# The spread of the output norm's roots as two full-width products, with its steps moved later in the dense work

## The chip, the cores and the metric

The kernel runs on one core of a Trainium2 chip. The metric is the device time of one execution in microseconds (us), as a median of several executions. All arithmetic is in 32-bit floats; a matmul that must be nearly exact in fp32 is written as three products of "high" and "low" parts in the faster type fp32r.

## The reference

One layer of a hybrid encoder is applied to a prompt of 2048 tokens and to a sample of 512 tokens, each with 16 meta tokens ahead of it:

```
u = RMSNorm(h);  proj = u @ w_in          # q, k, v, z of two branches, two merge gates
o_a = neighbourhood attention (8 rows x 16 columns of a 64-wide grid, 2-D bias)
o_b = window attention (+-128 tokens, grouped queries, T5 bias, a sink per head)
y_a = (o_a * silu(z_a)) @ w_proj_a;  y_b = (o_b * silu(z_b)) @ w_proj_b
h   = h + (sigmoid(g_a) * y_a + sigmoid(g_b) * y_b) @ w_out
out = RMSNorm(h)[without the meta tokens]  # x * rsqrt(mean(x*x) + 1e-6) * final_g
```

The change concerns the last line: the sums of squares of h for each token, the root of each, and the multiplication of h by it. The width of h is 1024.

## The kernel before, in words

The 2560 tokens are cut into five windows of 512 (window 0 is the sample). The first part of the kernel, up to about 1190 us, makes all projections, with most of their products in a scheme of seven instead of eight block products, and stores q, k, v, z and the gates in DRAM. The second part, which the change touches, runs over `units` of attention: for each window 32 units of branch a and then 16 of branch b. A unit has stages, and each pass of the main loop takes one unit's loads, another's scores (`s`, lines 1117 and 1118 for branch a, 1223 and 1224 for b), the normalisation of a third (`pr` and `prs`, lines 1058 to 1065), the transposes of a fourth (`tp`, lines 1141, 1243 and 1246, whose results are split into `ph` on ScalarE and `pl` on VectorE, lines 1144/1145 and 1250/1251) and the products with v of a fifth (`oa` and `ob`).

Between these stages TensorE does the dense work, in small steps: a generator yields after each six matmuls of 512 columns (lines 146 to 148). `fill(share)` takes as many steps as are due: one before and one after a unit's transposes in branch b, one per pass in branch a. Steps that a phase has left over are carried into the next (`chain`). The phases are, for each window w:

- beside branch a of window w: `dense_pb(w-1)` (16 steps, tile `psb`, with the loaded gates `sgb`), then `dense_out(w-1)` for the first four of eight output tiles (16 steps, `pso`);
- beside branch b of window w: `dense_out(w-1)` for the last four (16 steps), then `dense_pa(w)` (16 steps, `psa`, gates `sga`), and woven into these by `with_fill` the generator `dense_fin(w-1)`.

`dense_out` leaves for each output tile f the sum h times final_g in `hT`, and adds the square of h into `ssq` on GpSimd (line 1359). `dense_fin(w)`, which runs four times, then makes the norm: `sums` multiplies four 128-token pieces of `ssq` with a column of ones (TensorE, line 170, into the PSUM tile `fin_v`), `rsqrt` finds the roots for 128 x 4 tokens in some 13 small VectorE instructions (lines 153 to 163), `diagonal` puts them on four 128 x 128 diagonals (VectorE, line 177), `spread` multiplies ones with these so that every partition holds all 512 roots (TensorE, line 185, into the PSUM tile `rs_rb`), ScalarE copies them to `rbs` (line 1369), and GpSimd multiplies the eight `hT` by `rbs` (line 1373), each followed by a store to the output through SP's DMA queue.

TensorE's order is the order in which the program issues its instructions (a manual schedule). The other engines and SP's queue are ordered by a planner that simulates the kernel while it builds it. PSUM tiles of one tag share slots: the tag `tp` has three, and serves the transposes (two tiles for a unit of b with three key blocks, one for a unit of a), the scores of every third unit of a, `fin_v` and `rs_rb`. A new tile of a tag waits until all readers of the slot's old tile are done. The gate, residual and output-gate tiles (`sg`) have three slots in SBUF.

After the last unit `finish_end` does the last window's `psb` and its output product `pse`, token-major, with `w_out` halves (`woh`, `wol`) that it loads at that point through SP's queue.

Of the kernel before, what the change touches and what calls it, by code (L numbers as in the profile page):

```python
# [9 lines left out]
F32 = mybir.dt.float32  # L10
F32R = mybir.dt.float32r
# [6 lines left out]
P = 128  # L18
# [7 lines left out]
WTOK = 512  # L26
# [69 lines left out]
def encoder_block(ctx: ExitStack, tc: tile.TileContext, xT, x_end, w_in, w_pa, w_pb, w_o, norm_g, final_g,  # L96
                  final_row, bias_a0, bias_a1, bias_a2, bias_a3, bias_b, bias_b0, outT_p, outT_s, out_e):
    nc = tc.nc
# [23 lines left out]
    def f32(ap):  # L122
        return ap.bitcast(F32)
# [17 lines left out]
    def move(out, in_):  # L141
        last_move[0] = nc.sync.dma_start(*(f32(a) if a.dtype == F32R else a for a in (out, in_)))
        return last_move[0]
# [6 lines left out]
    def rsqrt(small, sq, m, nc_):  # L150

        ve, hv, r, t = (small.tile([P, 8], F32, tag=f"rs{i}", name=f"rs{i}")[:m, :nc_] for i in range(4))
        nc.vector.tensor_scalar(ve, sq, 1.0 / D_MODEL, EPS, ALU.mult, ALU.add)
        nc.vector.tensor_scalar(r.bitcast(I32), ve.bitcast(I32), 1, None, ALU.arith_shift_right)
        nc.vector.tensor_scalar(r.bitcast(I32), r.bitcast(I32), -1.0, float(0x5F3759DF), ALU.mult, ALU.add)
        nc.vector.tensor_scalar(hv, ve, -0.5, None, ALU.mult)
        for _ in range(3):
            if nc_ == 1:
                nc.vector.scalar_tensor_tensor(t, r, hv, r, ALU.mult, ALU.mult)
            else:  # L160
                nc.vector.tensor_mul(t, r, hv)
                nc.vector.tensor_mul(t, t, r)
            nc.vector.scalar_tensor_tensor(r, t, 1.5, r, ALU.add, ALU.mult)
        return r

    def sums(ssq, c0, m, nc_, psum, tag):

        v = psum.tile([P, WTOK], F32, tag=tag, name="fin_v")
        for c in range(nc_):
            nc.tensor.matmul(v[:m, c : c + 1], ssq[:, c0 + c * m : c0 + (c + 1) * m], ones[:, 0:1],  # L170
                             start=True, stop=True)
        return v[:m, :nc_]

    def diagonal(dg, r, m, eng=nc.vector):

        nc_ = r.shape[1]
        eng.tensor_mul(dg[:m, : nc_ * m].rearrange("p (c n) -> p c n", n=m),
                             ident[:m, None, :m].broadcast_to([m, nc_, m]),
                             r[:m, :, None].broadcast_to([m, nc_, m]))

    def spread(psum, tag, dg, m, nc_):

        rb = psum.tile([P, WTOK], F32, tag=tag, name="rs_rb")
        for c in range(nc_):
            nc.tensor.matmul(rb[:, c * P : c * P + m], ones[:m, :], dg[:m, c * m : c * m + m], start=True, stop=True)
        return rb

    def by_ones(psum, tag, h, l, name):

        v = psum.tile([P, WTOK], F32, tag=tag, name=name)  # L190
        nc.tensor.matmul(v, ones_r, h, start=True, stop=False)
        nc.tensor.matmul(v, ones_r, l, start=False, stop=True)
        return v
# [1090 lines left out]
    pools = {}  # L1284
# [7 lines left out]
    def open_dense():  # L1292
        last.close()
        for i, name, bufs in ("d", "dn", 2), ("m", "mp", 1):
            pools[i] = ctx.enter_context(tc.tile_pool(name=name, bufs=bufs, side="right", reuse_waits="tile"))
# [8 lines left out]
    def dense_pa(w):  # L1304
        yh, yl = ys["a", w]
        for f in range(KT):
            if f % 2 == 0:
                wt = weights.next()
            sg = gated("sga", g_d["a", w, f])
            ps = ps_d.tile([P, WTOK], F32, tag="d", name="psa")  # L1310
            for k in range(4):
                s = slice((4 * (f % 2) + k) * P, (4 * (f % 2) + k + 1) * P)
                mm3(ps, wt[:, 0, s], wt[:, 1, s], yh[:, k, :], yl[:, k, :], k == 0, k == 3)
                if k % 2:
                    yield
            ta = acc["t", w, f] = pools["m"].tile([P, WTOK], F32, tag=f"mh{f}", name="ta")
            nc.vector.tensor_mul(ta, ps, sg)

    def dense_pb(w):
        yh, yl = ys["b", w]  # L1320
        acc["m", w] = []
        for f in range(KT):
            if f % 2 == 0:
                wt = weights.next()
            sg = gated("sgb", g_d["b", w, f])
            ps = ps_d.tile([P, WTOK], F32, tag="d", name="psb")
            for k in range(4):
                s = slice((4 * (f % 2) + k) * P, (4 * (f % 2) + k + 1) * P)
                mm3(ps, wt[:, 0, s], wt[:, 1, s], yh[:, k, :], yl[:, k, :], k == 0, k == 3)
                if k % 2:  # L1330
                    yield
            nc.vector.tensor_mul(sg, ps, sg)
            nc.gpsimd.tensor_add(sg, sg, acc["t", w, f])
            mh, ml = (pools["m"].tile([P, WTOK], F32R, tag=f"m{i}{f}", name=f"m{i}") for i in "hl")
            acc["m", w].append((mh, ml))
            nc.scalar.copy(mh, sg)
            nc.gpsimd.tensor_sub(ml, sg, f32(mh))

    def dense_out(w, fs):
        if fs[0] == 0:  # L1340
            acc["s", w] = pools["d"].tile([P, WTOK], F32, tag="ssq", name="ssq", bufs=1)
        ssq = acc["s", w]
        for f in fs:
            wt = weights.next()
            x = gated("xres", xT[f * P : (f + 1) * P, w * WTOK : (w + 1) * WTOK])
            ps = ps_d.tile([P, WTOK], F32, tag="d", name="pso")
            for k in range(KT):
                s = slice(k * P, (k + 1) * P)
                mm3(ps, wt[:, 0, s], wt[:, 1, s], *acc["m", w][k], k == 0, k == KT - 1)
                if k % 2:  # L1350
                    yield
            hT = acc["h", w, f] = pools["m"].tile([P, WTOK], F32, tag="hT", name="hT", bufs=8)
            nc.vector.tensor_add(hT, ps, x)
            nc.scalar.activation(x, hT, AF.Square)
            nc.scalar.mul(hT, hT, fg[:, f : f + 1])
            if f == 0:
                nc.gpsimd.tensor_copy(ssq, x)
            else:
                nc.gpsimd.tensor_add(ssq, ssq, x)

    def dense_fin(w):
        r = rsqrt(pools["d"], sums(acc["s", w], 0, P, 4, ps_p, "tp"), P, 4)
        dg = pools["d"].tile([P, WTOK], F32, tag="rbs", name="rs_dg", bufs=1)
        diagonal(dg, r, P)
        for _ in range(5):
            yield
        rb = spread(ps_p, "tp", dg, P, 4)
        rbs = pools["d"].tile([P, WTOK], F32, tag="rbs", name="rbs", bufs=1)
        nc.scalar.copy(rbs, rb)
        for f in range(KT):  # L1370
            hT = acc["h", w, f]
            with tc.issue_after(low[0]):
                nc.gpsimd.tensor_mul(hT, hT, rbs)
            dst = outT_s if w == 0 else outT_p
            c0 = 0 if w == 0 else (w - 1) * WTOK
            move(dst[f * P : (f + 1) * P, c0 : c0 + WTOK], hT)
            yield
# [98 lines left out]
    def with_fill(main, fill):  # L1476

        for _ in main:
            yield
            next(fill, None)  # L1480
        for _ in fill:
            yield

    def phases(w, br):

        if br == "a":
            if w == 0:
                yield from islice(gates, GATES_A)
            else:
                yield from dense_pb(w - 1)  # L1490
                yield from dense_out(w - 1, range(0, 4))
        elif w == 0:
            yield from gates
            open_dense()
            yield from dense_pa(0)
        else:
            yield from dense_out(w - 1, range(4, 8))
            pa = dense_pa(w)
            yield from islice(pa, 1)
            yield from with_fill(pa, dense_fin(w - 1))  # L1500


# [27 lines left out]
    ps_p = ctx.enter_context(tc.tile_pool(name="ps_p", bufs=3, space=PSUM))  # L1530
# [9 lines left out]
    with tc.manual_schedule(engines={E.PE}):  # L1540
# [22 lines left out]
        for i in range(N):  # L1563
            br, w, _, weight = units[i]
# [128 lines left out]
```

## Time and profile before

| what | value |
|---|---|
| median of 3 runs | 1886.56 us (1884.48 to 1887.48) |
| the profiled execution's own time | 1884.6 us |
| its span in the profile | 1882.6 us |
| TensorE busy | 1857.5 us (99%) |
| VectorE busy | 1326.1 us (70%) |
| ScalarE busy | 1144.5 us (61%) |
| GpSimd busy | 729.2 us (39%) |
| mean granted TensorE clock | 0.998 |
| DMA | 414.35 MB, mean 220 GB/s |

In the profile PE is TensorE's matmuls and PEld its weight loads, DVE is VectorE, ACT ScalarE, POOL GpSimd, and SP issues the DMAs. A row of a timeline has the start in us from the span's start, the duration, the engine, the line of the kernel, the operation, the tiles out<-in, and in brackets how long the engine was idle before it and what ended that. A matmul's recorded duration overlaps the next one's, so the price of a matmul is read from start to start.

### The profile page before, as it was taken

How to read it: one execution, taken by the hardware profiler on the slowest of the kernel's cores; microseconds unless marked ns; L12 is line 12 of the kernel's file. 1: busy time of each engine (PE TensorE's matmuls, PEld its weight loads, DVE VectorE, ACT ScalarE, POOL GpSimd, SP SyncE). 2: the span in 40 equal slices, each digit the busy share in tenths (PEclk: the TensorE clock that was granted, in tenths of full speed). 3: DMA queues.
4: the chain of work that ended last, by engine and by line, in shares of the span. 5: the costliest groups of instructions: out<-in, count | busy, mean ns of one | idle time of the engine just before them, and what ended most of it. 6: DMA issues, size and time to landing. Idle time of an engine off the chain costs nothing. (4 is left out here: it accounts for less than half of the span.)

```text
span 1882.6 us, 29816 instructions
## 1 busy us (share of the span) xinstructions
PE 1857.5 (99%) x9797; PEld 1585.1 (84%) x9797; DVE 1326.1 (70%) x2961; ACT 1144.5 (61%) x2528; POOL 729.2 (39%) x558
## 2 busy tenths in 40 slices
PE   8999999999999999999999999999999999999998
PEld 6988888888888888888888888888888888888887
DVE  8985667556477565544457888878887877888874
ACT  6444444434365444444456797797789778878932
POOL 2005343323203222322324435656744763685420
PEclk9999999999999999999999999999999999999999
DMA  7675666655295677644259878977986997697483
GB/s 262 199 195 183 194 184 182 209 188 179 84 341 185 189 216 199 208 139 160 104 187 316 274 221 265 305 213 249 319 275 187 316 307 227 218 315 259 118 301 133
DMA packets 288145, 414.35 MB, mean 220 GB/s; under 512 B 117736, under 2 KB 162360, under 8 KB 286456
## 3 DMA queue, kind: packets, MB, share of 16 engines
q1 hardware_dynamic: 287704, 412.45, 68.1%
q8 instruction: 78, 1.28, 0.3%
q14 instruction: 75, 0.61, 0.1%
q10 hardware_dynamic: 288, 0.01, 0.0%
HBM read 303.46 MB, written 108.91 MB: 219 GB/s over the span
## 5 line engine op out<-in xcount | busy, mean ns | idle before, releaser
L208 POOL TENSOR_TENSOR wt<-wraw,wt 128x512 fp32r<-128x512 f32 x164 | 213.0, 1317 | 266.9 <-ACT wt L207 266.8
L850 PE MATMUL pa<-u,wt 128*128 128x512 f32 x1008 | 244.5, 392 | 2.1 <-ACT wt L207 1.1
L850 PE MATMUL pa<-u,x 128*128 128x512 f32 x984 | 236.7, 389 | 0.4 <-ACT u L861 0.4
L850 PEld LDWEIGHTS pa<-u,wt 128*128 128x128 f32 x1008 | 189.9, 189 | 42.4 <-ACT wt L207 1.5
L207 ACT CAST wt<-wraw 128x512 fp32r<-128x512 f32 x312 | 178.0, 619 | 74.8 <-PE mm L148 29.8
L850 PEld LDWEIGHTS pa<-u,x 128*128 128x128 f32 x984 | 184.5, 188 | 39.2 <-ACT u L861 0.8
L821 POOL TENSOR_TENSOR s<-wraw,raw 128x512 f32<-128x512 f32 x40 | 58.2, 1456 | 279.4 <-DVE x L208 279.4
L146 PE MATMUL mm<-u,wt 128*128 128x512 f32 (+2 forms) x416 | 150.4, 362 | 7.1 <-ACT u L334 7.1
L816 POOL TENSOR_TENSOR s<-raw 128x512 f32<-128x512 f32 x40 | 58.1, 1454 | 232.8 <-DMA raw<-in_w_in_dram 116.0
L147 PE MATMUL mm<-u,wt 128*128 128x512 f32 (+2 forms) x416 | 146.8, 353 | 1.1 <-DVE u L335 1.1
L148 PE MATMUL mm<-u,wt 128*128 128x512 f32 (+2 forms) x416 | 146.6, 352 | 0.0
L208 DVE TENSOR_TENSOR wt<-wraw,wt 128x512 fp32r<-128x512 f32 x148 | 104.5, 744 | 52.3 <-ACT wt L207 52.1
L850 PE MATMUL pe<-u,wt 128*128 128x512 f32 x504 | 121.4, 390 | 0.0
L850 PE MATMUL pc<-u,wt 128*128 128x512 f32 x504 | 121.1, 389 | 0.0
L850 PE MATMUL pe<-u,x 128*128 128x512 f32 x480 | 115.3, 389 | 0.0
L850 PEld LDWEIGHTS pe<-u,wt 128*128 128x128 f32 x504 | 94.6, 188 | 19.6
L850 PEld LDWEIGHTS pc<-u,wt 128*128 128x128 f32 x504 | 94.6, 188 | 19.6
L1145 DVE TENSOR_TENSOR pl<-tp,ph 128x384 fp32r<-128x384 f32 (+6 forms) x160 | 94.9, 593 | 20.9 <-ACT ph L1144 18.7
L1144 ACT CAST ph<-tp 128x384 fp32r<-128x384 f32 (+6 forms) x160 | 81.5, 510 | 43.0 <-PE tp L1141 41.4
L146 PE MATMUL pso<-mh,wt 128*128 128x512 f32 x256 | 107.1, 418 | 0.0
L829 POOL TENSOR_TENSOR s<-wraw,s 128x512 f32<-128x512 f32 x40 | 54.0, 1350 | 136.3 <-DVE wt L208 136.3
L850 PEld LDWEIGHTS pe<-u,x 128*128 128x128 f32 x480 | 90.1, 188 | 18.7
(258 smaller groups left out, 5024.8 us busy)
## 6 DMA issues: line engine op xcount, KB each, us to landing
wraw<-in_w_in_dram SPq DMA_DIRECT2D x86, 512.0 KB
raw<-in_w_in_dram SPq DMA_DIRECT2D x40, 512.0 KB
q<-qa SPq DMA_DIRECT2D x40, 512.0 KB
wraw<-in_w_o_dram SPq DMA_DIRECT2D x32, 512.0 KB
kbt<-kb SPq DMA_DIRECT2D x32, 384.0 KB
qa<-evq SPq DMA_DIRECT2D x20, 512.0 KB
qb<-evq SPq DMA_DIRECT2D x20, 512.0 KB
ka<-evk SPq DMA_DIRECT2D x20, 512.0 KB
```

The costliest lines, as they stand in the source:

```text
L146: nc.tensor.matmul(ps, wh, uh, start=first, stop=False)
L147: nc.tensor.matmul(ps, wh, ul, start=False, stop=False)
L148: nc.tensor.matmul(ps, wl, uh, start=False, stop=last)
L207: nc.scalar.copy(h, r)
L208: low[0] = (eng or lo_eng[0]).tensor_sub(l, r, f32(h)).ins
L816: eng.tensor_add(s1, a21, a22)
L821: eng.tensor_sub(s3, a11, a21)
L829: eng.tensor_sub(s4, a12, s2)
L850: nc.tensor.matmul(ps, wt[:, a, s], u[:, b, kk, :], start=first and kk == 0 and i == 0, stop=kk == 3 and i == 2, skip_group_check=True)
L1144: nc.scalar.copy(ph_[:kb, a], tb)
L1145: nc.vector.tensor_sub(pl_[:kb, a], tb, f32(ph_[:kb, a]))
```

## The change

In `dense_fin` the roots are split into a high part in fp32r and the rest, and two sets of diagonals are built instead of one (the second in the slot of `ssq`, whose last reader is `sums`). The spread becomes two products of 512 columns (`by_ones`) instead of four fp32 products of 128 columns. Seven steps are waited between the sums and the spread instead of five. In `phases` the generator starts after two steps of `dense_pa` instead of one.

```diff
     def dense_fin(w):
         r = rsqrt(pools["d"], sums(acc["s", w], 0, P, 4, ps_p, "tp"), P, 4)
-        dg = pools["d"].tile([P, WTOK], F32, tag="rbs", name="rs_dg", bufs=1)
-        diagonal(dg, r, P)
-        for _ in range(5):
+        rh, rl = (pools["d"].tile([P, 8], F32R, tag=f"r{x}", name=f"r{x}", bufs=1)[:, :4] for x in "hl")
+        nc.vector.tensor_copy(rh, r)
+        nc.vector.tensor_sub(rl, r, f32(rh))
+        dh, dl = (pools["d"].tile([P, WTOK], F32R, tag=tag, name=f"rs_{tag}", bufs=1) for tag in ("rbs", "ssq"))
+        diagonal(dh, f32(rh), P)
+        diagonal(dl, f32(rl), P)
+        for _ in range(7):
             yield
-        rb = spread(ps_p, "tp", dg, P, 4)
+        rb = by_ones(ps_p, "tp", dh, dl, "rs_rb")
         rbs = pools["d"].tile([P, WTOK], F32, tag="rbs", name="rbs", bufs=1)
...
             pa = dense_pa(w)
-            yield from islice(pa, 1)
+            yield from islice(pa, 2)
             yield from with_fill(pa, dense_fin(w - 1))
```

The two helpers that spread, old and new (both were in the kernel before):

```python
    def spread(psum, tag, dg, m, nc_):
        rb = psum.tile([P, WTOK], F32, tag=tag, name="rs_rb")
        for c in range(nc_):
            nc.tensor.matmul(rb[:, c * P : c * P + m], ones[:m, :], dg[:m, c * m : c * m + m], start=True, stop=True)
        return rb

    def by_ones(psum, tag, h, l, name):
        v = psum.tile([P, WTOK], F32, tag=tag, name=name)
        nc.tensor.matmul(v, ones_r, h, start=True, stop=False)
        nc.tensor.matmul(v, ones_r, l, start=False, stop=True)
        return v
```

## The prediction, made before the change was run

> **What bounds the kernel now.** I read the page first, then the waits of TensorE's loads after 1190 us (where the four norms lie), then the timelines around each norm.
>
> ```profile
> span 1882.6 us, 29816 instructions
> PE 1857.5 (99%) x9797; PEld 1585.1 (84%) x9797; DVE 1326.1 (70%) x2961; ACT 1144.5 (61%) x2528; POOL 729.2 (39%) x558
> ...
> PEld fin_v L170 <- POOL ssq L1359: 1.9, 4, 0.5
> PEld ob L1267 <- issue: 0.9, 1, 0.9
> ```
>
> TensorE is busy 99% of the span: a microsecond counts only if it is TensorE's own work or a hole in its stream. The second part of the fence holds such holes: the four sums wait 1.9 us in all for the last square to be added on GpSimd. The change can win that, and whatever the spread becomes cheaper; it can lose by new holes. The profiled execution took 1884.6 us, 2.0 more than its span, and lies 2.0 below the median of 1886.56. About 0.2% (3.8 us) is what a measurement of this kernel can tell from no change.
>
> **The sums, one step later.** Timeline of PE and POOL: the last transpose ahead of the sums, the sums, the second dense matmul after them; the same neighbours without sums; and the sums of the last norm.
>
> ```profile
> 1277.26 1.28 POOL L1359 TENSOR_TENSOR ssq<-ssq,xres 128x512 f32<-128x512 f32 x1
> 1278.07 0.27 PE L1246 MATMUL tp<-ident,prs 128*32 128x128 f32 x1
> 1278.60 1.05 PE L170 MATMUL fin_v<-ones,ssq 128*128 128x1 f32 x8 [0.26 <-POOL ssq L1359]
> 1279.83 0.40 PE L147 MATMUL psa<-ya,wt 128*128 128x512 f32 x1
> ...
> 1284.58 0.27 PE L1246 MATMUL tp<-ident,prs 128*32 128x128 f32 x1
> 1284.93 0.40 PE L147 MATMUL psa<-ya,wt 128*128 128x512 f32 x1
> ...
> 1780.70 0.27 PE L1246 MATMUL tp<-ident,prs 128*32 128x128 f32 x1
> 1782.21 0.40 PE L147 MATMUL psa<-ya,wt 128*128 128x512 f32 x1
> ```
>
> GpSimd ends the last addition at 1277.26 + 1.28 = 1278.54, and the sums start at 1278.60. With sums the stretch L1246 to L147 takes 1.76 us in the first norm and 1.51 in the last; without, 0.35. The sums' own eight passes cost about 0.89 (as the spread's eight below), so the holes are 1.76 - 0.35 - 0.89 = 0.52 and 0.27; the two norms between are like the first. One dense step later the addition is some 2.7 us old (a step: sums at 1278.60, spread at 1292.36, five steps between, 2.75 each). Term: 0.5 + 0.5 + 0.5 + 0.3 = **-1.8 us**, bounds -1.9 (the whole row above) and 0 (GpSimd late by a further step). The place itself costs nothing: no PSUM slot is asked for between old and new place.
>
> **The spread as two products.**
>
> ```profile
> 1292.36 1.05 PE L185 MATMUL rs_rb<-rs_dg,ones 128*128 128x128 f32 x8
> ...
> 1293.48 0.39 PE L147 MATMUL psa<-ya,wt 128*128 128x512 f32 x1
> 1293.71 0.40 PE L148 MATMUL psa<-ya,wt 128*128 128x512 f32 x1
> ...
> L191 PE MATMUL rs_rb<-rs_dg,ones x2: 392/393/394, 307.0 to 307.5; 128*128 128x512 f32 x2
> L192 PE MATMUL rs_rb<-rs_dg,ones x2: 392/396/400, 307.3 to 307.7; 128*128 128x512 f32 x2
> ```
>
> Four fp32 products are eight passes. From their start to the second dense matmul are 1.12 us; one dense matmul is 0.23 (1293.71 - 1293.48), so the spread holds TensorE 0.89. The new form stands in the first part of this very kernel: four such products start at 307.0, 307.3, 307.5 and 307.7, thus 0.23 to 0.24 each, 0.46 for two. Term: 4 x (0.89 - 0.46) = **-1.7 us**; bounds -2.0 and -1.4, by 0.07 of rounding in each norm.
>
> **VectorE's additions.** A copy and a subtraction of 128x4 and a second diagonal, in each norm.
>
> ```profile
> L162 DVE TENSOR_TENSOR rs<-rs,rs x12: 151/161/1143, 1282.0 to 1786.9; 128x4 f32<-128x4 f32 x12
> L177 DVE TENSOR_TENSOR rs_dg<-ident,rs x4: 684/684/693, 1287.4 to 1788.1; 128x512 f32<-128x512 f32 x4
> 1285.00 1.14 DVE L162 TENSOR_TENSOR rs<-rs,rs 128x4 f32<-128x4 f32 x1
> 1284.82 2.54 POOL L208 TENSOR_TENSOR wt<-wraw,wt 128x512 fp32r<-128x512 f32 x2 [6.27 <-ACT wt L207]
> ```
>
> That is 0.16 + 0.16 + 0.68 = 1.0 us, or up to 3 more if each falls on a GpSimd instruction as the one at 1285.00 did. The old diagonal was ready at 1287.4 + 0.7 = 1288.1, 4.3 us ahead of the spread at 1292.36; the new one has two more steps (5.5 us), so the cover grows. Term 0; VectorE's other work, which gets 1.0 us less room, is charged to the range.
>
> **The spread's new place.** It moves by three steps: one from the start, two from the wait. In the program's order the first norm's spread then comes right behind the transposes of the last unit of branch b; below, those transposes, the scores of the next unit, and who reads them.
>
> ```profile
> 1297.62 0.40 PE L1117 MATMUL s<-kd,q 128*128 128x512 f32 x1
> 1299.49 0.82 PE L1243 MATMUL tp<-ident,prs 128*128 128x128 f32 x6
> 1300.14 0.27 PE L1246 MATMUL tp<-ident,prs 128*32 128x128 f32 x1
> 1301.33 1.02 DVE L1251 TENSOR_TENSOR pl<-tp,ph 128x512 fp32r<-128x512 f32 x2
> 1301.46 0.70 ACT L1063 ACTIVATE pr<-s,rd 128x512 f32<-128x512 f32 x1
> ```
>
> All three slots of `tp` are then taken: one by these scores (the second unit of branch a, one of those whose scores are in `tp`), read until 1301.46 + 0.70 = 1302.2, two by the transposes, the first read until about 1301.33 + 0.7 = 1302.0. TensorE would be there at 1300.25 and has to wait: **+1.8 us**, once. Bounds: +1.1 (the readers start at once: transposes end, 0.4 on ScalarE, 0.6 on VectorE) and +2.5. The leftover step of each phase carries one step into the next window, so the other norms' spreads come at other places: behind the first unit of branch a (slots free by these rows 0.2 us earlier), behind the second, and behind the last unit. I take **+0.3** for them; bounds 0 and +1.5.
>
> **The multiplications and the stores.** The carried steps change no work: after the last unit eight dense steps follow where five did. But in each norm GpSimd's eight multiplications and eight stores of 256 KB move by some 8 us, and SP's queue with them.
>
> ```profile
> 1297.42 1.58 SPq L142 DMA_DIRECT2D out_dram<-hT  x2
> 1302.42 4.08 SPq L142 DMA_DIRECT2D out_dram<-hT  x4
> 1306.59 0.38 SPq L142 DMA_DIRECT2D sgb<-gb  x1
> ...
> 1300.00:1305.00 5.00, 5.00 (x32) 4.30 (x31) 4.02 (x12) 3.83 (x10) 5.00 (x5) 1.00 0.66 175
> 1305.00:1310.00 5.00, 5.00 (x33) 4.40 (x32) 3.83 (x13) 4.16 (x10) 5.00 (x5) 1.00 1.00 328
> ...
> 1523.46 0.69 DVE L1332 TENSOR_TENSOR sgb<-psb,sgb 128x512 f32<-128x512 f32 x1 [2.91 <-DMA sgb<-gb]
> 1525.49 0.52 PE L1141 MATMUL tp<-ident,pr 128*128 128x128 f32 x3 [1.87 <-DVE pr L1065]
> ```
>
> In the windows' rows the last two columns are the DMA share and GB/s. Until 1305 the DMA engines have room (0.66), from then on none (1.00). A store that leaves the first stretch for the second makes the loads later; such lateness does reach TensorE: at 1523.46 VectorE had waited 2.91 us for a gate, and TensorE lost 1.87. On the other side, the loads from 1306.59 on stand right behind four stores that wait for GpSimd, and would go earlier without them. Which of the two wins no row shows: bounds -1.9 (the hole at 1525 gone) and +7.6 (rival C); as the rows speak for both, I take 0.
>
> The Trainium skill, "DMA: Bandwidth & Descriptors", section "Issuing engines are not separate DMA queues", says that all DMAs end on the same 16 engines and interleave there. The share of 1.00 agrees; by that rule the 2 MB of a norm's stores cost the loads the same wherever the engines are full, which is rival C and not the 0 taken here.
>
> **The end.**
>
> ```profile
> 1794.98 12.29 POOL L1373 TENSOR_TENSOR hT<-hT,rbs 128x512 f32<-128x512 f32 x8 [14.05 <-ACT rbs L1369]
> 1796.41 3.36 DVE L208 TENSOR_TENSOR wt<-wraw,wt 128x512 fp32r<-128x512 f32 x2
> 1801.41 0.36 PE L1267 MATMUL ob<-ph,vb 128*128 128x256 f32 x1 [0.47 <-DVE y L1277]
> ...
> 1810.00:1820.00 10.00, 10.00 (x46) 8.29 (x45) 6.77 (x11) 3.26 (x6) 0.00 (x0) 1.00 0.98 390
> ...
> L1434 PE MATMUL pse<-woh,mh x72: 278/389/390, 1830.9 to 1874.4; 128*128 128x512 f32 x56, 128*128 128x256 f32 x16
> L1424 DVE TENSOR_TENSOR ml<-sgb,mh x8: 682/684/693, 1817.6 to 1838.7; 128x512 fp32r<-128x512 f32 x8
> ```
>
> Today GpSimd's multiplications run beside VectorE's weight splits; two take 3.36 us instead of 2 x 0.68 (the like diagonal above), and TensorE then waits for VectorE at 1801.41. They leave this place: **-0.6** (between the 0.9 of the waits' row and 0.47 of this one); bounds -0.9 and 0. The Trainium skill, "SBUF — State Buffer", section "Who interferes with whom", has it that a VectorE instruction with two SBUF inputs is blocked by a GpSimd one that reads SBUF. The rows agree, and by that rule the blocking would fall on later splits instead: the sum would lose the 0.6.
>
> They go to where `finish_end` loads: DMA share 0.98 at 390 GB/s. Six dense steps of 1.4 us follow the new spread, so multiplications of 1.3 to 1.5 us put about three stores behind that seam, where one is now: 0.5 MB more, 1.3 us at 390 GB/s. The last `ml` ends at 1838.7 + 0.7 = 1839.4; TensorE reads it as 42nd matmul of `pse`, 1830.9 + 41 x 0.23 = 1840.3. Slack 0.9: **+0.4**; bounds 0 and +4.5 (all eight stores, 2.1 MB, 5.4 us, less the slack).
>
> **Sum:** -1.8 - 1.7 + 1.8 + 0.3 + 0 - 0.6 + 0.4 = -1.6 us, so 1883.0 against the profiled 1884.6, and 1885.0 against the median.
>
> **The rivals.**
>
> A, the forecast: gains and the slot's wait nearly cancel, 1885.0, within 0.2%.
>
> B, faster: the readers come early enough that the slots cost 1.1, and the loads that now stand behind the stores get ahead of them: -1.8 - 1.7 + 1.1 - 0.6 - 1.9 = -4.9, so 1881.7. For it speaks the row at 1306.59; against, that the stores then block others 8 us later.
>
> C, slower: the stores meet full DMA engines. The two at 1297 and some three of the four at 1302 are issued before 1305 now; 5 x 0.26 MB at 328 GB/s is 4.0 us, less what little room is left, 3.8. It decides where a gate is already waited for, as at 1523.46: from there each microsecond of lateness is TensorE's. In the windows beside branch a after the first and second norm that is 7.6, with the other terms +6.0: 1892.6. Against it: from 1305 to 1310, with full engines, TensorE is busy 5.00 of 5.00, and half of the price would stay within 0.2%.
>
> D, it does not do what it says: the sums wait at the new place too (GpSimd's queue holds the addition), +1.8 on A: 1886.8, no change.
>
> **How the numbers follow.** A 0.46, D 0.10, B 0.21, C 0.23. A and D are "same", 0.56; B beyond 3.8 is faster, 0.21; C slower, 0.23. The time is A's. The range takes in B less another 1.2 us, and most of C: 1880.5 to 1891.5. A's own range is 1882 to 1888.
>
> **What would show it.** The waits' row of `fin_v` for `ssq` is gone (D: it stays). The spread's two products stand 0.23 apart. In the first norm a hole of 1 to 2.5 us ahead of the spread, ended by a reader of `tp`. No wait at 1801 for VectorE. Holes of over 2 us in the stretches beside branch a, with VectorE waiting for `sgb`, speak for C; none there, not even that at 1525, for B. A hole in the middle of a stretch that the change does not touch would make the whole sum wrong: the planner may order the other engines anew.

## The result, and the profile after

The changed kernel takes 1898.31 us (median of 6 runs, 1895.77 to 1900.40); the kernel before, on the same chip, 1886.47. The ratio is 1.0064 with a 95% interval of 1.0050 to 1.0078: slower by 12 us, where a gain of 1.6 had been forecast. The profiled execution took 1898.94 us. In this document a ratio is turned into microseconds by 1886.

The head of the page of the changed kernel:

```profile
span 1896.7 us, 29800 instructions
...
PE 1862.9 (98%) x9773; PEld 1582.4 (83%) x9773; DVE 1330.5 (70%) x2975; ACT 1143.1 (60%) x2528; POOL 727.3 (38%) x556
```

The span grew by 14.1 us. TensorE has 24 records fewer (the spread's 32 passes became 8) and is recorded busy 5.4 us longer, so nothing is gained there and some 9 us are idle.

TensorE's waits from 1190 us on, matmuls first, then the weight loads' row for the sums (waited for, us in total, times, longest):

```profile
PE tp L1141 <- DVE pr L1065: 2.4, 4, 1.2
PE tp L1243 <- DVE pms L1261: 2.3, 2, 1.4
PE s L1117 <- DMA kd<-ka: 1.6, 1, 1.6
PE ob L1270 <- DVE pms L1261: 1.3, 2, 0.7
PE rs_rb L191 <- DVE pl L1251: 1.2, 1, 1.2
PE s L1223 <- ACT prs L1054: 1.2, 2, 0.6
PE s L1223 <- issue: 0.7, 1, 0.7
PE pse L1438 <- ACT mh L1427: 0.6, 1, 0.6
...
PEld fin_v L170 <- issue: 0.2, 1, 0.2
```

The sums' wait for `ssq`, 1.9 us before, is gone, as it should be. The first row is not new; before, it was

```profile
PE tp L1141 <- DVE pr L1065: 2.9, 4, 1.9
```

The rows below it are new: many waits of about a microsecond on other edges, for VectorE's `pms` and `pl` in the norms, and for loads and scores far from them. No single row carries 12 us.

The timeline of the first norm, TensorE (start, duration, and in brackets the idle time before):

```profile
1293.72 0.30 PE L1270 MATMUL ob<-pms,vms 96*64 96x128 f32 x2 [0.68 <-DVE pms L1261]
...
1302.11 0.41 PE L1243 MATMUL tp<-ident,prs 128*128 128x128 f32 x2 [0.91 <-DVE pms L1261]
1302.36 0.27 PE L1246 MATMUL tp<-ident,prs 128*32 128x128 f32 x1
1303.82 0.50 PE L191 MATMUL rs_rb<-rs_rbs,ones 128*128 128x512 f32 x1 [1.19 <-DVE pl L1251]
1304.16 0.39 PE L192 MATMUL rs_rb<-rs_ssq,ones 128*128 128x512 f32 x1
1304.39 0.40 PE L146 MATMUL psa<-ya,wt 128*128 128x512 f32 x1
1304.63 0.40 PE L147 MATMUL psa<-ya,wt 128*128 128x512 f32 x1
```

The spread stands behind the transposes and waits for a slot of `tp` that VectorE's `pl` still reads, as forecast: 1.46 us pass between 1302.36 and 1303.82. The transposes ahead of it waited too, 0.91 us for `pms`, which was not forecast. From the first product to the second dense matmul are 0.81 us, less one dense matmul of 0.23: the spread holds TensorE 0.58 instead of 0.89.

What the page can't show is why stretches that the change does not touch have holes. The experiments had to tell the change's parts apart: the form of the spread, the sums one step later, the spread behind transposes, the multiplications and stores three steps later, and the number of steps. That last part needs a word. `with_fill` runs one step of `dense_fin` behind each step of `dense_pa`. Before, 13 steps (5 of wait, 8 multiplications) went into 15 places. After it, 15 steps go into 14: one is left over, holds no matmul of its own, and takes a turn of the dense work when the next window has begun. From there on all dense work comes one step later beside the units, after the next norm two, and so on.

### The profile page after: what moved, and what is told of

Same layout as the page of the kernel before. It is cut to its first block, busy times and chain, and to the rows that moved or that the text cites. A ratio compares the mean times of both kernels' runs of the same rounds, so it can differ in the third digit from the quotient of the medians.

```text
span 1896.7 us, 29800 instructions
## 1 busy us (share of the span) xinstructions
PE 1862.9 (98%) x9773; PEld 1582.4 (83%) x9773; DVE 1330.5 (70%) x2975; ACT 1143.1 (60%) x2528; POOL 727.3 (38%) x556
## 4 chain that ended last, share of the span: by engine, by line
PE 79%; DMA 5%; DVE 4%; ACT 3%; issue 2%; POOL 1%; SPq 0%; POOLq 0%; DVEq 0%; ACTq 0%
PE pa L850 24%; PE pe L850 12%; PE pc L850 6%; PE pso L146 3%; PE pso L148 3%; PE pso L147 3%; PE tp L1141 2%; DMA sgb<-gb 2%; PE mm L146 2%; PE mm L148 2%; PE mm L147 2%; PE tp L1243 2%; PE oa L1156 1%; PE oa L1158 1%; PE s L1223 1%
## 5 line engine op out<-in xcount | busy, mean ns | idle before, releaser
L1054 ACT ACTIVATE s<-s,nm 128x384 f32<-128x384 f32 (+5 forms) x160 | 87.1, 544 | 37.3 <-DVE nm L1047 34.6
```

The source lines that it names most:

```text
L1054: nc.scalar.activation(out, s, AF.Exp, bias=nm, scale=-1.0, accum_out=sm)
```

## The experiments

All are timed against the kernel before on the same chip. Ratios stand with their 95% interval. The expectations, quoted as they were written before each run, name theories by letters or words; one letter can mean different things in different groups of runs.

### The form alone, and the tiles

`form_only` is the changed kernel with the old places:

```diff
-        for _ in range(7):
+        for _ in range(5):
...
-            yield from islice(pa, 2)
+            yield from islice(pa, 1)
```

> The kernel before with the new form alone: high and low diagonals and two products of 512 columns, at the old places (one step ahead, five steps between). VECTORE: the cheaper spread gives 1.7 and VectorE's 1.0 us more per norm costs one to two us in each: 1889 to 1892. SLOTS or LEFTOVER: 1886.5 - 1.7 = 1885. ADDRESSES adds up to 3.7 to either.

Measured: 1889.31, ratio 1.0021 [1.0009, 1.0032], +4.0 us. `form_old_tiles` is the same with the high and low roots in tiles that exist already, and `no_new_tiles` does only that to the changed kernel:

```diff
-        rh, rl = (pools["d"].tile([P, 8], F32R, tag=f"r{x}", name=f"r{x}", bufs=1)[:, :4] for x in "hl")
+        rh, rl = (pools["d"].tile([P, 8], F32R, tag=f"rs{i}", name=f"r{x}")[:, :4] for i, x in enumerate("hl"))
```

> The new form alone at the old places (which took 1889.3 against 1884.7), with the high and low roots in tiles that the pool has already, so that the dense matmuls' spacing after scores is 0.228 and not 0.232 us, as the run of the changed kernel with such tiles showed (its time stayed the same, the gain went into waits). ADDRESSES: 1889.3 - 3 = 1886. VECTORE (the holes come from VectorE's further work): 1889.

> The changed kernel, with the high and low roots in two tiles that the pool already has instead of two new ones: each engine's order of instructions is the changed kernel's, only addresses in SBUF differ. The changed kernel took 1898.3, 11.8 more than before. Its profile shows 14 us more than the old one's: about 11 more in holes of TensorE, 1.0 ahead of the units of attention, 3.7 in matmuls that start 0.233 instead of 0.227 us apart, less 1.7 for the spread. ADDRESSES (the two new tiles shift the pool and slow the operands' reads): 1894.5. Every other theory: 1898 within 2.

Measured: `form_old_tiles` 1886.12, 1.0005 [0.9996, 1.0014], +0.9 us, `no_new_tiles` 1898.44, 1.0069 [1.0054, 1.0084], no better than the changed kernel. TensorE, six dense matmuls that follow scores, first in `form_only`, then in `form_old_tiles`:

```profile
1265.60 0.39 PE L146 MATMUL pso<-mh,wt 128*128 128x512 f32 x1
...
1266.76 0.39 PE L148 MATMUL pso<-mh,wt 128*128 128x512 f32 x1
```

```profile
1267.25 0.39 PE L146 MATMUL pso<-mh,wt 128*128 128x512 f32 x1
...
1268.38 0.39 PE L148 MATMUL pso<-mh,wt 128*128 128x512 f32 x1
```

Five spacings take 1.16 us with the two new tiles of 32 bytes a partition and 1.13 without, 0.232 against 0.226 each. So the places of tiles in SBUF go with the matmuls' pace, but the total doesn't follow it clearly: 4.0 against 0.9 us in the form alone, 12.1 against 13.0 in the whole, and 5.7 against 3.4 in a third pair below, with intervals that overlap in all three. The form is not what costs 12 us; nor does it win the 1.7 that TensorE's own time suggested.

### The places alone, and each of them

`places_only` leaves the old spread and makes only the two moves (`range(7)`, `islice(pa, 2)`); `sums_later` only the second, `wait_seven` only the first.

```diff
-        for _ in range(5):           # places_only, wait_seven
+        for _ in range(7):
...
-            yield from islice(pa, 1)    # places_only, sums_later
+            yield from islice(pa, 2)
```

> The kernel before with the new places alone: sums one step later, seven steps between, old spread of four fp32 products with one set of diagonals. SLOTS and LEFTOVER: the sums' wait of 1.8 is won, the holes stay: 1893 to 1896. VECTORE: 1886.5 - 1.8 + 1.5 = 1886. ADDRESSES: 1886 or less, no new tile is there.

> The kernel before with the sums one dense step later and nothing else (five steps to the old spread, one set of diagonals); so the spread and the stores come one step later too, and no step is left over. The new places alone cost 13 us against a kernel before of 1884.7. SLOTS (what costs is that the spread waits for a slot of tp): the spread lies between two units' transposes with a slot free, the sums' wait of 1.8 is won: 1883. STORES (what costs is that GpSimd's multiplications and the 2 MB of stores of each norm run into the stretch with full DMA engines): a third of the way, 1884.7 - 1.8 + 4 = 1887.

> The kernel before with seven steps between sums and old spread, sums at the old place; no step is left over. The spread comes two steps later, one step after the last-but-one transposes of branch b. SLOTS: no slot is missing there, 1885 within 1.5. STORES: two thirds of the way, 1884.7 + 9 = 1893.

Measured: `places_only` 1898.12, 1.0072 [1.0058, 1.0086], +13.6 us: the places alone are the whole loss. `sums_later` 1887.83, 1.0010 [1.0000, 1.0020], +1.9; `wait_seven` 1886.63, 1.0006 [0.9997, 1.0015], +1.1. Each move alone costs next to nothing, and both together 13.6. What only both together do: 15 steps in 14 places leave one over (13 in 14 and 15 in 15 leave none), and the spread comes three steps later, behind transposes at a place where its slot of `tp` is still being read. Transposes ahead of it are not enough for that; in the first norm of `sums_later` the spread follows others at once:

```profile
1293.10 0.27 PE L1246 MATMUL tp<-ident,prs 128*32 128x128 f32 x1
1293.21 1.06 PE L185 MATMUL rs_rb<-rs_dg,ones 128*128 128x128 f32 x8
```

### The leftover step: a test that misled, and one that didn't

`no_leftover` leaves out the last empty `yield` of `dense_fin` in the changed kernel:

```diff
             move(dst[f * P : (f + 1) * P, c0 : c0 + WTOK], hT)
-            yield
+            if f < KT - 1:
+                yield
```

> The changed kernel, but dense_fin ends without a last yield, so that no step is left over and carried into the next window: dense steps and units meet as in the kernel before; the spread comes at the same place of the first norm (behind the last transposes of branch b) and so in all. LEFTOVER (the carried steps cause the holes beside branch a and in the later windows, some 6 us): 1892. SLOTS (the spread behind transposes waits for a slot of tp, 1.5 us in the first norm's profile, and now in three norms): 1898 to 1900. VECTORE (the second diagonal and the small instructions delay attention): 1898.

Measured: 1902.37, 1.0094 [1.0078, 1.0110]. It got worse, which seems to clear the leftover step. But without the carried step the later norms lie like the first, and the spread waits behind transposes in three norms (at 1301, 1474 and 1648 us) instead of one. A wait stands in this run that neither the kernel before nor the changed one has:

```profile
PE psb L147 <- POOL yb L1072: 3.7, 3, 1.5
```

The next window's dense work needs `yb`, which GpSimd splits behind the last five of its multiplications, and here it comes a turn earlier than in the changed kernel. So here the multiplications' new place does cost, where no carried step hides it. And behind two of the spreads the granted clock was 0.50 for 3.4 us (from 1476.0 and 1650.1), up to 1.7 us each. The test had taken one cost away and put others in.

`late_stores` keeps sums and spread where they were and puts three empty steps between the copy of the spread and the first multiplication. `empty_steps` puts the same three behind the last store, so that nothing is moved. `stores_late` leaves the multiplications too, and issues each store three steps after its multiplication. All three have 16 steps for 15 places: one is carried.

```diff
         nc.scalar.copy(rbs, rb)
+        for _ in range(3):      # late_stores
+            yield
...
             move(dst[f * P : (f + 1) * P, c0 : c0 + WTOK], hT)
             yield
+        for _ in range(3):      # empty_steps
+            yield
```

```diff
             nc.gpsimd.tensor_mul(hT, hT, rbs)    # stores_late
+            if f < 3:
+                yield
+                continue
+            hT, f = acc["h", w, f - 3], f - 3
...
             move(dst[f * P : (f + 1) * P, c0 : c0 + WTOK], hT)
             yield
+        for f in range(KT - 3, KT):
+            move(dst[f * P : (f + 1) * P, c0 : c0 + WTOK], acc["h", w, f])
+            yield
```

> The kernel before with sums and spread at their old places and three further steps between the copy of the spread and the first multiplication: only GpSimd's multiplications and the stores come as late as in the changed kernel (one step is left over, as there). SLOTS: 1885 within 1.5. STORES: 1884.7 + 10 or more, since the sums' wait is not won either: 1895 to 1899.

> The kernel before with three empty steps behind the last multiplication of each norm: nothing is moved, only more steps are left over for the next window. Theory S (the stores come late and meet full DMA engines): no difference from before, within 1.5 us. Theory E (the step that a phase leaves over shifts the next window's dense work, and that costs): what the multiplications with their stores three steps later cost, some +8.7 us.

> The kernel before with only the eight stores of each norm three steps later; sums, spread, copy and GpSimd's multiplications are where they were. Theory S (stores): +6 to +9 us, nearly all of the 8.7 that multiplications and stores moved together cost, with waits of TensorE for loads of branch a's and b's k. Theory M (GpSimd's multiplications at their new place slow VectorE or come ahead of other work of GpSimd): no difference, within 1.5 us. Theory E (steps left over): as for the empty steps, both at +8.7.

Measured: `late_stores` 1894.01, 1.0045 [1.0029, 1.0061], +8.5 us; `empty_steps` 1893.23, 1.0037 [1.0025, 1.0049], +7.0; `stores_late` 1891.40, 1.0030 [1.0019, 1.0042], +5.7. With nothing moved at all, the carried step costs as much, within the intervals, as with multiplications and stores three steps later. So the stores are not what costs. VectorE's waits for branch b's gates, the place where late loads were to show, first before, then after the change:

```profile
DVE sgb L1332 <- DMA sgb<-gb: 7.9, 4, 2.9
```

```profile
DVE sgb L1332 <- DMA sgb<-gb: 6.2, 6, 1.9
```

They shrank. TensorE's longest waits in `empty_steps` from 1190 us on:

```profile
PE tp L1141 <- DVE pr L1065: 2.8, 5, 0.8
PE s L1223 <- ACT prs L1054: 1.2, 2, 0.6
PE ob L1270 <- DVE pms L1261: 0.8, 1, 0.8
PE psa L146 <- ACT yb L1071: 0.6, 1, 0.6
PE s L1223 <- issue: 0.5, 1, 0.5
```

The first row is no larger than before (2.9); the others are new and small. One profiled execution can't tell where the carried step's 7 us lie, though. `end_27` and `end_33`, below, differ from the kernel before only in the last window, and up to 1720 us the instructions of every engine stand in the same order as before. Yet in their profiles the stretch from the first norm's sums to the last window's first product of branch b took 3.6 and 7.0 us longer than in the profile before, and in `end_27` the row is

```profile
PE tp L1141 <- DVE pr L1065: 5.8, 3, 2.6
```

### How the cost grows with the carried steps

`empty_four` has four empty steps instead of three (two carried in each norm), `one_carry` three behind the first norm alone (one carried, once).

```diff
+        for _ in range(4):                       # empty_four
+        for _ in range(3 if w == 0 else 0):      # one_carry
+            yield
```

> The kernel before with four empty steps behind the last multiplication of each norm: two steps are carried into the next window instead of the one of the kernel with three, so the windows 2, 3 and 4 run 2, 4 and 6 steps late instead of 1, 2 and 3. Theory P (parity: what costs is that each dense tile, two steps long beside branch a, ends in the other of two passes): 1885 to 1888, as before. Theory N (each carried step costs its share): twice the +7.6 of the three empty steps, 1898 to 1902. Theory O (the order comes out by chance better or worse): anything, and then no rule can be drawn.

> The kernel before with three empty steps behind the first norm alone: windows 2, 3 and 4 all run one step late. Theory P (parity): all three windows are at the odd place, where three empty steps in each norm had two of three there: +10 to +12, 1896 to 1898. Theory N (share for each step): 3 of the 6 window-steps, +3.8, 1889 to 1890. A cost of window 2 alone, where the holes of the kernel with three empty steps lay (1315 to 1380): about as that, +2.6 to +7.

Measured: `empty_four` 1897.60, 1.0060 [1.0047, 1.0073], +11.3 us; `one_carry` 1891.68, 1.0026 [1.0016, 1.0037], +4.9. An even number of steps is not free, so parity is out. Windows 2, 3 and 4 run late by 1, 1, 1 steps in `one_carry`, by 1, 2, 3 in `empty_steps`, by 2, 4, 6 in `empty_four`: 3, 6 and 12 window-steps for 4.9, 7.0 and 11.3 us. More steps cost more: 1.6, 1.2 and 0.9 us each, which may be falling or not, since each total is uncertain by some 2 us.

The last product of the last unit with v, and the last matmul of `psa`: before, in `empty_steps`, and in `empty_four`.

```profile
1801.95 0.28 PE L1272 MATMUL ob<-pl,vb 128*64 128x256 f32 x1
1809.41 0.39 PE L148 MATMUL psa<-ya,wt 128*128 128x512 f32 x1
```

```profile
1801.40 0.28 PE L1272 MATMUL ob<-pl,vb 128*64 128x256 f32 x1
1813.53 0.39 PE L148 MATMUL psa<-ya,wt 128*128 128x512 f32 x1
```

```profile
1803.74 0.28 PE L1272 MATMUL ob<-pl,vb 128*64 128x256 f32 x1
1820.00 0.39 PE L148 MATMUL psa<-ya,wt 128*128 128x512 f32 x1
```

The dense work behind the last unit grew from 7.5 to 12.1 and 16.3 us, three and six steps of 1.4 to 1.6. That much had been taken from beside the units. The first norm's sums start at 1278.60 before, and in both runs at

```profile
1276.38 1.05 PE L170 MATMUL fin_v<-ones,ssq 128*128 128x1 f32 x8 [0.27 <-POOL ssq L1359]
```

From there to the last product are 523.4 us before, and 525.0 and 527.4 here: 1.7 and 4.0 more, where 4.7 and 8.8 less had to come if TensorE had run through its remaining work sooner. So of the 6.3 and 12.8 us that these executions have lost at the last `psa`, 4.7 and 8.8 are deferred steps behind the last unit, and beside the units the profiles show nothing saved in return. (The 1.7 and 4.0 themselves are within what single executions differ by.)

`end_27` and `end_33` ask whether deferral is all: they change only the ration of dense steps beside the last window's branch b, so that three steps more or fewer stand behind the last unit, with no empty step.

```diff
-    COUNT = {..., ("b", NWIN - 1): 30}
+    COUNT = {..., ("b", NWIN - 1): 27}
```

> The kernel before with the dense steps beside the last window's branch b rationed by 27 instead of 30, so that three more steps (3 x 1.4 us) stand behind the last unit; no empty step anywhere. Theory U (dense work deferred past the last unit leaves holes beside the units, which do not run faster without it): +3 to +4, 1888 to 1890. Theory V (the order of the dense tiles against the units in the stretches beside branch a is what costs): no difference from before within 1.5 us.

> The same with 33 instead of 30: three steps fewer behind the last unit. Theory U: the units of the last window have holes to be filled, -1 to -3, 1883 to 1885, and a version faster than the kernel before. Theory V: no difference within 1.5 us, or slower if the last window's dense work comes ahead of what it needs.

Measured: `end_27` 1887.47, 1.0011 [1.0002, 1.0020], +2.1 us; `end_33` 1884.97, 0.9999 [0.9990, 1.0008], no difference. Three steps deferred from the last window's branch b cost 2.1 us [0.4, 3.8], between the two theories. In the profile of `end_27` the dense work behind the last unit is 4.7 us longer, as in `empty_steps`, and the products of that branch take 70.4 us instead of 72.8 from first to last: half of what is deferred is saved beside the units. In `empty_steps` the empty turns come when windows 2 to 4 begin, and the last window's products of branch b still take 72.8. So the two deferrals are not the same test, and why units beside an empty turn don't run sooner is open. A rival is untested: the planner orders the other engines anew for each program, and their recorded order in `empty_steps` leaves that of the kernel before at about 1320 us, so that a part of the 7 us may come from that order.

### The slot behind transposes, and the versions that avoid both

`form_four` is `form_old_tiles` with four steps of wait: one step earlier than before, nothing carried, and behind transposes in every norm. `after_six` is the changed kernel with six steps of wait, which leaves nothing over; `six_old_tiles` the same in existing tiles; `form_seven` is `form_old_tiles` with seven steps. Against the changed kernel:

```diff
-        for _ in range(7):           # stays in form_seven
+        for _ in range(6):           # after_six, six_old_tiles
+        for _ in range(4):           # form_four
...
-            yield from islice(pa, 2)
+            yield from islice(pa, 1)    # form_four, form_seven
```

> The new form in existing tiles, with four steps of wait instead of five and the sums at their old place: the spread is one step earlier than before, in the first norm right behind the transposes of a unit of branch b, and the stores leave one step earlier. Theory T (the slot costs 1.5 to 1.9, and VectorE's lateness behind it up to 2 more): 1.5 to 4 above the same form with five steps (1886.1), so 1887.6 to 1890, with a row of rs_rb waiting for pl or ph. If only the stores count (S alone): 1884 to 1886, not above the five steps, since no store comes later.

> The changed kernel with six steps of wait instead of seven, so that the spread and all behind it are two steps later than before, not three, and the first norm's spread does not stand behind transposes. Theory S with a threshold, and T (a slot of tp is waited for behind transposes): 1887 to 1890, since two steps alone gave 1886.6 and the new tiles cost some 3; no row of rs_rb waiting for pl. Theory S in proportion to the steps, without T: two thirds of the way, about 1894. If neither place matters and the whole is an order of the planner that comes out badly: anywhere up to 1898.

> The changed kernel with six steps of wait and the high and low roots in existing tiles: all of the change but the carried step, the spread behind transposes and the two new tiles. If carried step, slot and tiles are the whole of the loss: 1885 to 1889 (sums two units later cost +2, the form gains up to 1.7). If something else in the change costs: as with six steps and new tiles, 1892.

> The new form in existing tiles with seven steps of wait and the sums at their old place: the steps just fill the phase, so nothing is carried, and the first norm's spread stands behind scores, not transposes. Both steps that cost are avoided: 1885 to 1887. If the stores two steps later cost by themselves: 1888 and more. It beats the kernel before only if the two products' 1.7 us are not eaten by VectorE's additions, as they were with five steps (1886.1): 1883.5 to 1885.

Measured: `form_four` 1890.98, 1.0033 [1.0020, 1.0045], +6.2 us, against +0.9 one step later: 5.3 for four norms. TensorE's waits and the first norm's timeline:

```profile
PE rs_rb L191 <- DVE pms L1261: 6.9, 4, 1.8
...
1288.47 0.27 PE L1246 MATMUL tp<-ident,prs 128*32 128x128 f32 x1
1290.51 0.76 PE L191 MATMUL rs_rb<-rs_rbs,ones 128*128 128x512 f32 x1 [1.76 <-DVE pms L1261]
1291.07 0.63 PE L192 MATMUL rs_rb<-rs_ssq,ones 128*128 128x512 f32 x1
1291.50 0.63 PE L146 MATMUL psa<-ya,wt 128*128 128x512 f32 x1
1291.92 0.63 PE L147 MATMUL psa<-ya,wt 128*128 128x512 f32 x1
```

Four waits of 1.7 us each on average: the price of the place, with no store later than before. `after_six` 1891.93, 1.0030 [1.0018, 1.0041], +5.7, and `six_old_tiles` 1889.33, 1.0018 [1.0008, 1.0028], +3.4: one step less than the changed kernel gives back 6.4 and 8.7 us of its 12.1, about the carried step's share. The wait for a slot is not gone. It was expected to be, but with the spread behind scores it is 0.8 us in each of three norms, 2.5 in all (2.6 in `after_six`, against 1.2 in the changed kernel). What is left in `six_old_tiles`, its waits and the first norm:

```profile
PE rs_rb L191 <- DVE pl L1251: 2.5, 3, 1.0
...
PE ob L1270 <- DVE pms L1261: 2.0, 3, 0.7
...
1292.18 0.28 PE L1267 MATMUL ob<-ph,vb 128*128 128x256 f32 x1
1293.13 0.31 PE L1270 MATMUL ob<-pms,vms 96*64 96x128 f32 x2 [0.67 <-DVE pms L1261]
```

`pms` comes late in three norms. VectorE in the first norm, the diagonals and `pms` that follow the sums, before and after the change:

```profile
1287.42 0.69 DVE L177 TENSOR_TENSOR rs_dg<-ident,rs 128x512 f32<-128x512 f32 x1
...
1291.19 0.28 DVE L1261 TENSOR_TENSOR pms<-tp,pms 32x128 fp32r<-32x128 f32 x1
```

```profile
1292.02 0.69 DVE L177 TENSOR_TENSOR rs_rbs<-ident,rh 128x512 fp32r<-128x512 f32 x1
...
1293.29 0.28 DVE L1261 TENSOR_TENSOR pms<-tp,pms 32x128 fp32r<-32x128 f32 x1
1293.61 0.69 DVE L177 TENSOR_TENSOR rs_ssq<-ident,rl 128x512 fp32r<-128x512 f32 x1
```

Before, the diagonal was done 3.1 us ahead of `pms`; now the first diagonal lies right ahead of it, and `pms` is what TensorE waits for. `form_seven` avoids carried step, transposes and later sums, and measured 1889.58, 1.0022 [1.0012, 1.0032], +4.1: not the 1885 to 1887 expected. Its profile still has waits for `pl` in three norms, 1.0 us ahead of the spread and 1.6 ahead of transposes, but the profile is that of the fastest of the eleven executions (1885.36), so what made the others slower is not seen. No version beat the kernel before; `end_33`, `form_old_tiles` and `wait_seven` can't be told from it.

## Why the prediction was wrong, step by step

**The step that failed: "The carried steps change no work".** The leftover step was seen, and so was its trace at the end (eight dense steps after the last unit where there were five), and it was priced at nothing because the matmuls are the same. `empty_steps` shows +7.0 us [4.7, 9.2] for it with nothing else changed. The reasoning that equal work costs TensorE equal time leaves out that the 99% is kept by a supply of dense steps beside the units. What a turn without matmuls takes from there comes back behind the last unit (the eight steps instead of five, 11.7 us instead of 7.5 in the changed kernel's profile), and the units do not end sooner for it.

**The sums, -1.8.** The wait went (1.9 to 0.2), the gain didn't come: `sums_later` is +1.9 [0.0, 3.8]. The root's small VectorE instructions moved with the sums, and one step later they and the diagonal lie ahead of `pms`. In the first norm of `sums_later` two short holes, 0.3 us ahead of the next products with v and 0.2 ahead of the product with `pms`, stand where the kernel before has none; with the second diagonal (`six_old_tiles`) the latter is 0.67. The prediction followed TensorE's and GpSimd's side of the move and not VectorE's. That these holes are the whole of the missing gain is not shown.

**The spread as two products, -1.7.** Mis-sized: 0.58 us in the new form, not 0.46, as the first product stands 0.34 from the second (1303.82 to 1304.16), so 4 x 0.31 = -1.2. In the time even that did not show: +0.9 [-0.8, 2.6] in existing tiles.

**VectorE's additions, 0.** True at the old place within the interval just given; with the sums one step later the copy, the subtraction and the first diagonal lie ahead of `pms` (the 0.68 us ahead of 1293.72 in the first norm).

**The slot of `tp`, +1.8 in the first norm.** Right: 1.46 between the rows, inside the bounds of 1.1 and 2.5, and 1.7 in each norm of `form_four`. The **+0.3** for the other norms was not needed: the row of `rs_rb` has one entry.

**Multiplications and stores, 0.** The stores: right, though the kernel got slower. Rival C, the only one on the slower side, gave 1892.6 by stores that meet full DMA engines. `stores_late` differs from `empty_steps` by -1.3 us with intervals that overlap, and the gates' waits shrank from 7.9 to 6.2. Who had bet on C would have come nearer to the time for a reason that isn't so. The multiplications: the changed kernel shows no wait for `yb` behind them, but `no_leftover`, where `psb` comes a turn earlier, waits 3.7 us, so their delay is hidden in the one and costs in the other.

**The end, -0.6 and +0.4.** The wait for `y` at 1801 is gone from its place, and `pse` waits 0.6 for `mh`, both as said. The second was sized too small: from the last `psa` to the end are 74.6 us instead of 73.2, so 1.4 and not 0.4. `wait_seven` has 1.1 of it, which is as much as its whole loss.

Summed from the separate runs: carried step +7.0, sums +1.9, two steps of wait +1.1, the slot once 1.5, together 11.5, against 13.6 [10.9, 16.2] in `places_only`, which has these parts alone, and 12.1 in the whole. Each term has some 2 us of uncertainty and they need not be additive, so the sum shows the order of size and no more.

What stays open: why the units gain nothing from the dense steps that a carried step takes from beside them. Shown are that it costs, that more carried steps cost more, that parity is not the reason, and that in the profiles the deferred steps are paid behind the last unit. Where the rest of the loss lies, and what the planner's new order has to do with it, is not shown.

## What to carry to other kernels

In a hand-ordered stream, count the steps before and after a change: a step more than the phase has places for shifts everything that follows, and that is a change by itself, to be priced by a run with empty steps. Before an instruction is moved, follow the small work that hangs on it on every engine, not only the wait that is to go. And when a test of one cause gets slower, see whether it has moved something else into a bad place before the cause is cleared.

## What the runs showed of the hardware

A hole of TensorE can be followed by a slower clock, and so go with a loss of more than its length. In `form_four` the 2.0 us between 1288.47 and 1290.51 are followed by matmuls 0.43 us apart (1291.07, 1291.50, 1291.92 above) instead of 0.23. The windows of that stretch (us, busy of PE, PEld, DVE, ACT, POOL, then granted clock, DMA share, GB/s):

```profile
1288.00:1290.50 2.50, 0.55 (x3) 0.29 (x4) 2.40 (x10) 1.94 (x6) 0.00 (x0) 0.96 1.06 410
1290.50:1294.00 3.50, 3.49 (x9) 2.78 (x10) 2.19 (x6) 2.17 (x7) 1.60 (x2) 0.54 1.01 375
1294.00:1296.00 2.00, 2.00 (x16) 1.83 (x14) 0.70 (x3) 0.38 (x2) 2.00 (x2) 1.00 0.94 366
```

The granted clock is 0.54 for 3.5 us: seven matmuls at 0.20 more, so 1.4 us on top of the hole. It did not come each time: behind the like holes of this kernel's other norms (2.0 us at 1460 and 1631) the matmuls kept their 0.23. The Trainium skill, "TensorE: Matmul & The Clock Gate", section "Why this matters for your kernels", asks to keep idle gaps of TensorE below some 3 us; here a hole of 2.0 had the clock halved once in three, and in `no_leftover` holes of 1.5 us and less were followed by the 0.50 named above.

The other surprise is the pace of matmuls by the place of tiles: 0.232 against 0.226 us behind scores, with two tiles more of 32 bytes a partition that no matmul reads. Why is not shown.
